# Opening of a hybrid encoder block: left halves of the first row tiles first, idle transposes between them, one operand split straight from PSUM, two differences on another engine

## The chip, the cores and the metric

The kernel runs on one core of one Trainium2 chip. The time is that of one execution on the device, in microseconds (us), and a kernel's time is the median of its runs. Five engines work beside each other: PE (TensorE, matrix products and transposes, with PEld for its weight loads), DVE (VectorE), ACT (ScalarE), POOL (GpSimd) and SP (SyncE, which here issues most of the transfers). Each carries out its own queue of instructions in order. PE writes to PSUM, which has eight banks of 128 x 512 float32 here; DVE and ACT read them, POOL does not.

## The reference

One encoder layer on 1024 tokens of width 1024. The change touches the input norm and the first columns of the combined projection.

```python
h = layer_norm(x, ln_in_g, ln_in_b)
for l in range(DEPTH):
    proj = h @ w_in[l]
    aq, ak, av, hq, hf_fwd, hf_bwd, hi, hg, ga, gh = jnp.split(proj, split_idx, axis=-1)
    att = dilated_attention(aq, ak, av, slopes)
    rec = hgrn2(hq, hf_fwd, hf_bwd, hi, hg, lower_bounds[:, l], hgrn_norm_g[l])
    merged = jax.nn.sigmoid(ga) * (att @ w_att_up[l]) + jax.nn.sigmoid(gh) * (rec @ w_hgrn_up[l])
    h = layer_norm(DEEPNORM_ALPHA * h + merged @ w_o[l], ln1_g[l], ln1_b[l])
    gate, up = jnp.split(h @ w_ffn_in[l], 2, axis=-1)
    h = layer_norm(DEEPNORM_ALPHA * h + (jax.nn.silu(gate) * up) @ w_ffn_out[l], ln2_g[l], ln2_b[l])
```

## The kernel before

**Products.** Every float32 operand of a product is split into a rounded high part and the rest, `hi` and `lo`, and a product is three matmuls: `w_hi` by `hi`, `w_hi` by `lo`, `w_lo` by `hi` (`mm3`, lines 270, 271 and 272 of the profile). A big product is done by Strassen's and Winograd's scheme with seven products of half size instead of eight. The projection's right operand is the normalised input, transposed, in four quarters: `b11` (features 0 to 511, tokens 0 to 511), `b21` (features 512 to 1023, same tokens), `b12` and `b22` (tokens 512 to 1023). Besides `b11`, `b21` and `b22` the scheme needs `t1` = b12 - b11, `t2` = b22 - t1, `t3` = b22 - b12 and `t4` = b21 - t2. Each is held as `xb11hi`, `xb11lo` and so on, in four slices of 128 features (k = 0 to 3). On the weights' side it needs the blocks a11 to a22 and their sums s1 to s4 (`sums`, lines 652 to 657: s1 = a21 + a22 and s2 = s1 - a11 on DVE, s3 = a22 - s2 on POOL, s4 = a12 - s2 on DVE).

**Order of the products.** `stream` makes the columns in groups of four tiles of 128, n = 0, 1, ...; a group has two halves g = 0, 1, and each of its seven products, numbered p = 1 (a11, b11), 2 (a12, b21), 6 (s2, t2), 5 (s1, t1), 7 (s3, t3), 3 (s4, b22) and 4 (a22, t4), takes 12 matmuls. The first two groups start together: p = 1 for n = 0 and 1, then p = 2 for both, and only then the rest of n = 0, then of n = 1. So p = 2 has four "b21 groups" of 12 matmuls: (n, g) = (0, 0), (0, 1), (1, 0), (1, 1). `prep` splits a product's weight, `w_hi` on ACT (line 212) and `w_lo` on POOL (line 222), three products ahead, into a ring of four; `leave` evacuates: `wkeep` copies on ACT (line 680), sums and `evh` on DVE and ACT (lines 542, 543, 556 to 558).

**The opening.** `phase0` makes the right operands while `stream`'s products run. Per row tile of 128 tokens (tt = 0 to 7, tile `xt`): `stats` on DVE (lines 348 to 350) and three small instructions on POOL (lines 351 to 353, tile `mv`), `norm` in place, half a row (q = 0 left, q = 1 right) per ACT instruction (line 331), `turn`, which transposes 128 x 128 pieces on PE (line 364) so that one PSUM bank (`sd`, four of them) gets one slice k of four row tiles. From these banks come: `w11`, the scaled b11 without its bias (`scaled`, line 376 on DVE, 331 on ACT), split to `b11`; `w21` (tile `v21`), split to `b21`; for the later four row tiles `t1` = bank - w11 (`less`, line 380, DVE), `z2` = bank - t1 and a scaled copy `w22` (ACT) from the right halves' banks; then the splits of t2 and t1, t3's difference (line 467, POOL, into w11's place), the splits of t3 and of b22 (both from SBUF), t4's difference (line 482, POOL) and its split. `hi` is an ACT instruction, `lo` a DVE instruction (lines 390, 391). `lent` names tiles that borrow the place of operands which are not made yet.

**What sets the order.** A scheduler orders each engine's queue by the place in the program and by priorities (evacuations ahead). Where `ordered` and `behind` are called, one instruction is held behind another in its queue without a wait: `xact` and `xdve` keep ACT's and DVE's instructions of the first half of the opening in the order written, and `gates` holds the first four weight casts behind given instructions. `run` lets `stream` go on by one product, so that its instructions stand there.

## Time and profile before

| | us |
|---|---|
| three runs | 2061.17, 2062.42, 2066.87 |
| median | 2062.42 |
| the profiled execution's own time | 2064.15 |
| its span | 2062.3 |
| first matmul of a product | 17.00 |
| first matmul of the second column group's p = 6 | 88.04 |

Rows of the timeline have the start in us, the time in us from the first one's start to the last one's end, engine, line, operation, what is written and read, shapes, the count of instructions merged, and in brackets how long the engine had been idle and what released it. An instruction's time holds the way through the engine too: matmuls of 0.39 us follow each other every 0.23 us. Rows of stages have the stretch, its length, the busy time (and count) of PE, PEld, DVE, ACT and POOL, the clock granted to PE as a share of the full one, the busy share of the DMA engines and GB/s.

### The profile page before, as it was taken

What the parts mean: (1) busy time and instruction counts of PE and PEld (TensorE: products, weight loads), DVE (VectorE), ACT (ScalarE), POOL (GpSimd) and SP (SyncE); (2) the same over time, 40 slices, a digit from 0 to 9 for tenths busy, and PEclk for the clock granted to TensorE, in tenths of its full rate; (3) what the DMA queues carried; (4) which work ended last, traced back from release to release, by engine and by line L of the source; (5) the groups of instructions that cost most, each with busy time, mean ns of one, the idle gap of its engine ahead of it and who ended that gap; (6) DMA issues with size and microseconds to landing.
All of it is one profiled execution on the core that took longest, in us unless ns stands there. A gap on an engine that the chain in (4) does not pass through costs nothing. (4 is left out here: it accounts for less than half of the span.)

```text
span 2062.3 us, 30940 instructions
## 1 busy us (share of the span) xinstructions
PE 2015.5 (98%) x10974; PEld 1670.5 (81%) x10974; DVE 1326.1 (64%) x2029; ACT 947.6 (46%) x1962; POOL 1063.9 (52%) x913
## 2 busy tenths in 40 slices
PE   7899999999999999999999999999999999999998
PEld 5688888788888888888888888787888888888886
DVE  6867645884377844677443225547777777767788
ACT  6554455553555536555365432244433333344541
POOL 5767644676446663666535652244656666630000
PEclk9999999999999999999999999999999999999999
DMA  5434533335334353344524376544544344358533
GB/s 158 133 115 142 171 119 105 128 129 177 116 127 132 114 177 98 121 131 145 165 95 150 123 247 204 183 133 125 171 131 141 127 149 137 108 170 298 160 96 128
DMA packets 274843, 297.94 MB, mean 144 GB/s; under 512 B 14017, under 2 KB 207362, under 8 KB 274690
## 3 DMA queue, kind: packets, MB, share of 16 engines
q1 hardware_dynamic: 268384, 274.78, 41.6%
q10 hardware_dynamic: 6306, 21.20, 2.7%
q8 instruction: 86, 1.41, 0.3%
q14 instruction: 67, 0.55, 0.1%
HBM read 201.29 MB, written 94.63 MB: 143 GB/s over the span
## 5 line engine op out<-in xcount | busy, mean ns | idle before, releaser
L222 POOL TENSOR_TENSOR w_lo<-wa,w_hi 128x512 fp32r<-128x512 f32 x272 | 362.6, 1341 | 274.7 <-ACT w_hi L212 259.7
L212 ACT CAST w_hi<-wa 128x512 fp32r<-128x512 f32 x272 | 168.4, 620 | 253.5 <-PE pj L271 146.8
L222 POOL TENSOR_TENSOR w_lo<-wsum,w_hi 128x512 fp32r<-128x512 f32 x88 | 128.0, 1464 | 111.7 <-PE sd L272 60.7
L222 POOL TENSOR_TENSOR w_lo<-f_raw,w_hi 128x512 fp32r<-128x512 f32 x66 | 102.5, 1561 | 53.2 <-ACT w_hi L212 51.8
L208 POOL TENSOR_TENSOR mv<-mv,mhalf 128x1 f32<-128x1 f32 x16 | 12.7, 797 | 218.9 <-DVE mv L207 218.1
L212 ACT CAST w_hi<-wsum 128x512 fp32r<-128x512 f32 x88 | 54.7, 621 | 122.2 <-PE sd L271 118.7
L542 DVE TENSOR_TENSOR evh<-wkeep,pj 128x512 f32<-128x512 f32 x45 | 30.9, 686 | 111.9 <-PE pj L272 63.2
L212 ACT CAST gwsum<-a_raw 128x512 fp32r<-128x512 f32 (+1 forms) x78 | 48.2, 618 | 112.6 <-PE pj L271 56.1
L270 PE MATMUL pj<-xt1hi,w_hi 128*128 128x512 f32 x252 | 99.6, 395 | 0.0
L270 PE MATMUL pj<-xb22hi,w_hi 128*128 128x512 f32 x252 | 99.1, 393 | 0.0
L272 PE MATMUL pj<-xb22hi,w_lo 128*128 128x512 f32 x252 | 98.2, 390 | 0.4 <-POOL w_lo L222 0.3
L271 PE MATMUL pj<-xb22lo,w_hi 128*128 128x512 f32 x252 | 98.6, 391 | 0.0
L272 PE MATMUL pj<-xt1hi,w_lo 128*128 128x512 f32 x252 | 98.5, 391 | 0.0
L271 PE MATMUL pj<-xt1lo,w_hi 128*128 128x512 f32 x252 | 98.4, 391 | 0.0
L654 POOL TENSOR_TENSOR wa<-wa,wa 128x512 f32<-128x512 f32 x46 | 67.1, 1467 | 40.4 <-DVE wa L653 35.5
L222 POOL TENSOR_TENSOR w_lo<-ws,w_hi 128x512 fp32r<-128x512 f32 x46 | 62.4, 1358 | 43.3 <-ACT w_hi L212 43.0
L680 ACT COPY wkeep<-pj 128x512 f32<-128x512 f32 x136 | 79.3, 583 | 7.8 <-PE pj L272 5.7
L531 DVE TENSOR_TENSOR evh<-wkeep,pj 128x512 f32<-128x512 f32 x66 | 57.8, 879 | 35.6 <-PE pj L272 25.1
L272 PE MATMUL pj<-xt2hi,w_lo 128*128 128x512 f32 x192 | 76.1, 396 | 4.1 <-POOL w_lo L222 4.1
L270 PE MATMUL pj<-xt2hi,w_hi 128*128 128x512 f32 x192 | 76.4, 401 | 1.1 <-ACT w_hi L212 1.1
L270 PE MATMUL pj<-xt4hi,w_hi 128*128 128x512 f32 x192 | 76.1, 396 | 0.8 <-ACT w_hi L212 0.8
L270 PE MATMUL pj<-xb11hi,w_hi 128*128 128x512 f32 x192 | 76.9, 402 | 0.0
(419 smaller groups left out, 6546.5 us busy)
## 6 DMA issues: line engine op xcount, KB each, us to landing
wa<-in_w_in_dram SPq DMA_DIRECT2D x184, 256.0 KB, 3.3
f_raw<-in_w_ffn_in_dram SPq DMA_DIRECT2D x44, 512.0 KB, 4.2
a_raw<-gd SPq DMA_DIRECT2D x30, 512.0 KB, 3.7
gd<-fc SPq DMA_DIRECT2D x44, 256.0 KB, 2.1
gd<-fs SPq DMA_DIRECT2D x33, 256.0 KB, 2.1
tg<-evh SPq DMA_DIRECT2D x32, 256.0 KB, 2.2
tg<-tg SPq DMA_DIRECT2D x16, 512.0 KB, 3.9
y<-ahs SPq DMA_DIRECT2D x16, 512.0 KB, 6.5
```

What stands on the lines that cost most here:

```text
L208: nc.gpsimd.tensor_tensor(mv[:, 2:3], mv[:, 2:3], self.mhalf[:, 0:1], OP.pow)
L212: ins = nc.scalar.copy(hi, src) if eng_hi == "act" else nc.vector.tensor_copy(hi, src)
L222: ins = e.tensor_sub(lo, src, hi.bitcast(F32))
L270: nc.tensor.matmul(ps, whi, xhi, start=first, stop=False, **kw)
L271: nc.tensor.matmul(ps, whi, xlo, start=False, stop=False, **kw)
L272: self.product = nc.tensor.matmul(ps, wlo, xhi, start=False, stop=last, **kw).ins.name
L531: self.left(nc.vector.tensor_tensor(o, self.order_src(add, g, kind), s, OP.add))
L542: self.left(nc.vector.tensor_add(t, add, ps))
L654: nc.gpsimd.tensor_sub(a["a21"], a["a22"], a["a11"])
L680: nc.scalar.copy(t, ps)
```

## The change

The opening alone is changed. In the loop over the first four row tiles only the first tile's right half is normalised on ACT; those of tiles 1 to 3 are written after the loop and go to DVE, as do the left halves of tiles 6 and 7 later. The first two weight casts are held behind the left-half norms of tiles 1 and 2. Between the left-half transposes stand 11, 7, 6 and 4 transposes of the identity into a place of a bank that is written later (`run_up`). The norms of tiles 4 to 7 are written left halves first. From each bank of tiles 4 to 7's left halves ACT now also copies the scaled b12 (`w12`); t3's difference is bank - w12 on DVE. b22 is split from PSUM: ACT writes its high part from the bank, then that part less the bias (`hb`, with `nbin`, the negated bias, made on POOL in the padding tile), and DVE writes the low part from bank and `hb`. t4's difference is on DVE. The sums s1 and s2 (and s3) of the first group's weights are put behind the first two slices of t1 (`later`).

```diff
@@ phase0
-        w11, t1, w22, z2 = (lent(z) for z in ("xb22hi", "xt3hi", "xt4hi", "xt4lo"))
+        w11, w12, t1, hb, z2 = (lent(z) for z in ("xb22hi", "xt4hi", "xt3hi", "xt3lo", "xt4lo"))
+        WARM = (11, 7, 6, 4)
+        nbin = self.spare[:, 0:4]
...
         def norm(tt, q):
             x, mv = xs[tt][:, HALF * q:HALF * (q + 1)], self.mv0[:, tt, :]
+            if tt > 5 and q == 0 or 0 < tt < 4 and q:
+                return dve(nc.vector.tensor_scalar(x, x, mv[:, 2:3], mv[:, 3:4], op0=OP.mult, op1=OP.add))
             return act(x, x, AF.Identity, bias=mv[:, 3:4], scale=mv[:, 2:3])
...
+        def run_up(n):
+
+            for i in range(n):
+                if 3 not in banks:
+                    banks[3] = self.ps_sd()
+                ins = nc.tensor.transpose(banks[3][:, 384:512], self.ident, self.ident)
+                if i == 0 and self.turned_last:
+                    self.behind(ins, self.turned_last)
+                self.turned_last = ins.ins.name
...
+        self.gates = [None] * 2
         for tt in range(4):
-            norm(tt, 0)
+            n = norm(tt, 0)
+            if 0 < tt < 3:
+                self.gates[tt - 1] = n.ins.name
+            run_up(WARM[tt])
             turn(tt, 0)
             if tt < 3:
                 stats(tt + 1)
+            if tt == 0:
                 norm(tt, 1)
+        for tt in range(1, 4):
+            norm(tt, 1)
         bias = [[column("bin", 4 * q + k) for k in range(4)] for q in range(2)]
+        nc.gpsimd.tensor_scalar(nbin, self.col["bin"][:, 4:8], -1.0, None, op0=OP.mult)
...
-        norm(3, 1)
         stats(4)
-        self.gates = [None] * 2 + [h.ins.name] * 2
+        self.gates += [h.ins.name] * 2
...
-        for tt in range(4, 8):
-            norm(tt, 0)
-            if tt < 7:
-                stats(tt + 1)
-            norm(tt, 1)
+        for tt in range(5, 8):
+            stats(tt)
+        for q in range(2):
+            for tt in range(4, 8):
+                norm(tt, q)
+        self.later = []
         run(3)
         for k in (0, 2):
             for tt in range(4, 8):
                 turn(tt, 0, (k, k + 1))
             for i in (k, k + 1):
-                less(t1, i, 0, w11)
+                scaled(w12, i, 0, True)
+                self.left(less(t1, i, 0, w11))
+            if k == 0:
+                for z in self.later:
+                    z()
+                self.later = None
             run()
+        self.forms("b22")
         for k in (0, 2):
...
             for i in (k, k + 1):
                 h = hi("t2", i, z2, bias[1][i]), lo("t2", i, z2, bias[1][i])
-                scaled(w22, i, 1, True)
+                parts.append(h)
+            for i in (k, k + 1):
+                ins = less(w12, i, 1, w12)
+                if i > k:
+                    self.behind(ins, parts[0][1].ins.name)
+                g, b, z = column("gin", 4 + i), bias[1][i], self.xb["b22"][0][:, i, :]
+                self.behind(act(z, banks[i], AF.Identity, bias=b, scale=g), h[0].ins.name)
+                act(hb[i], z.bitcast(F32), AF.Identity, bias=nbin[:, i:i + 1])
+                dve(nc.vector.scalar_tensor_tensor(self.xb["b22"][1][:, i, :], banks[i], g, hb[i], op0=OP.mult,
+                                                   op1=OP.subtract))
             run()
...
-        for k in range(4):
-            self.behind(nc.gpsimd.tensor_sub(w11[k], z2[k], w11[k]), last.ins.name)
...
-            hi("t3", k, w11, diff[:, k:k + 1])
-            last = lo("t3", k, w11, diff[:, k:k + 1])
-        run(2)
-        self.forms("b22")
+            hi("t3", k, w12, diff[:, k:k + 1])
+            last = lo("t3", k, w12, diff[:, k:k + 1])
+        run(3)
         for k in range(4):
-            hi("b22", k, w22, bias[1][k])
-            lo("b22", k, w22, bias[1][k])
-        run()
-        for k in range(4):
-            self.behind(nc.gpsimd.tensor_sub(w21[k], w21[k], z2[k]), last.ins.name)
+            self.behind(nc.vector.tensor_sub(w21[k], w21[k], z2[k]), last.ins.name)
@@ stream, sums
             n, g, p = seq[i]
             a = A[g]
+            if n == 0 and p == 6 and self.later is not None and not again:
+                self.later.append(lambda: sums(i, True))
+                return
```

How the queues stand where the prediction speaks of them. Line numbers of the changed kernel are its own (there line 372 is `turn`, 383 `run_up`).

PE's queue from the start of the program, before and with the change. `vrows` is the transpose of the norm's parameters, rows with `xt` are row tiles, rows without it the identity.

```order
L181 MATMUL sd<-tabs_sb,vrows_256 128x16
L364 MATMUL sd<-tabs_sb,xt 128x128 x22
L270 MATMUL pj<-xb11hi,w_hi 128x512 x2
L364 MATMUL sd<-tabs_sb,xt 128x128 x3
L271 MATMUL pj<-xb11lo,w_hi 128x512
```

```order
L183 MATMUL sd<-tabs_sb,vrows_257 128x16
L383 MATMUL sd<-tabs_sb 128x128 x11
L372 MATMUL sd<-tabs_sb,xt 128x128 x4
L383 MATMUL sd<-tabs_sb 128x128 x7
L372 MATMUL sd<-tabs_sb,xt 128x128 x4
L383 MATMUL sd<-tabs_sb 128x128 x6
L372 MATMUL sd<-tabs_sb,xt 128x128 x4
L383 MATMUL sd<-tabs_sb 128x128 x4
L372 MATMUL sd<-tabs_sb,xt 128x128 x12
L272 MATMUL pj<-xb11hi,w_hi 128x512 x2
L372 MATMUL sd<-tabs_sb,xt 128x128 x4
L273 MATMUL pj<-xb11lo,w_hi 128x512
```

28 transposes of the identity are added; of the right halves' transposes eight, not six, stand ahead of the first product.

POOL's queue from the last statistic of the third row tile to the first weight splits, before and with the change (`mv` is the statistic, three instructions a tile).

```order
L353 TENSOR_SCALAR mv_203<-mv_203 128x1
L351 TENSOR_SCALAR mv_203<-mv_203 128x1
L352 TENSOR_TENSOR mv_203<-mv_203,mhalf 128x1
L353 TENSOR_SCALAR mv_203<-mv_203 128x1
L222 TENSOR_TENSOR w_lo<-wa_259,w_hi 128x512
L222 TENSOR_TENSOR w_lo<-wa_261,w_hi 128x512
```

```order
L358 TENSOR_SCALAR mv_203<-mv_203 128x1
L356 TENSOR_SCALAR mv_203<-mv_203 128x1
L357 TENSOR_TENSOR mv_203<-mv_203,mhalf 128x1
L224 TENSOR_TENSOR w_lo<-wa_260,w_hi 128x512
L358 TENSOR_SCALAR mv_203<-mv_203 128x1
L224 TENSOR_TENSOR w_lo<-wa_262,w_hi 128x512
```

The first weight split now stands ahead of the last statistic of the fourth row tile.

DVE's queue from the evacuation of the second b21 group (`wkeep<-wkeep,sd`), before and with the change. `lent_xt4lo` is z2, `lent_xt3lo` hb, and `lent_xt4hi` holds w12 and then t3's difference.

```order
L556 TENSOR_TENSOR wkeep<-wkeep,sd 128x512
L380 SCALAR_TENSOR_TENSOR lent_xt4lo<-sd,vc,lent_xt3hi 128x512 x2
L558 SCALAR_TENSOR_TENSOR evh<-evh,wkeep 128x512
L391 SCALAR_TENSOR_TENSOR xt2lo<-lent_xt4lo,vc,xt2hi 128x512 x2
L556 TENSOR_TENSOR wkeep<-wkeep,sd 128x512
L380 SCALAR_TENSOR_TENSOR lent_xt4lo<-sd,vc,lent_xt3hi 128x512 x2
```

```order
L401 SCALAR_TENSOR_TENSOR lent_xt4lo<-sd,vc,lent_xt3hi 128x512
L596 SCALAR_TENSOR_TENSOR evh<-evh,wkeep 128x512
L594 TENSOR_TENSOR wkeep<-wkeep,sd 128x512
L412 SCALAR_TENSOR_TENSOR xt2lo<-lent_xt4lo,vc,xt2hi 128x512
L401 SCALAR_TENSOR_TENSOR lent_xt4hi<-sd,vc,lent_xt4hi 128x512
L401 SCALAR_TENSOR_TENSOR lent_xt4lo<-sd,vc,lent_xt3hi 128x512
L401 SCALAR_TENSOR_TENSOR lent_xt4hi<-sd,vc,lent_xt4hi 128x512
L412 SCALAR_TENSOR_TENSOR xt2lo<-lent_xt4lo,vc,xt2hi 128x512
L401 SCALAR_TENSOR_TENSOR lent_xt4lo<-sd,vc,lent_xt3hi 128x512
L596 SCALAR_TENSOR_TENSOR evh<-evh,wkeep 128x512
L504 SCALAR_TENSOR_TENSOR xb22lo<-sd,vc,lent_xt3lo 128x512
L412 SCALAR_TENSOR_TENSOR xt2lo<-lent_xt4lo,vc,xt2hi 128x512
```

The second piece begins behind three instructions that are not shown: the evacuation `wkeep`, a z2 and a t3 difference (in w12's place). With them the first `xb22lo` is the fourteenth instruction from that `wkeep` on, where before it was far outside this stretch; b22's bank is read until then.

More of the change, by code (lines that the diff above doesn't have):

```diff
@@ L125, in pad @@
         if n:
-            self.nc.gpsimd.memset(pool.tile([128, n // 4], F32, name=f"pad{n}"), 0.0)
+            t = pool.tile([128, n // 4], F32, name=f"pad{n}")
+            self.nc.gpsimd.memset(t, 0.0)
+            return t
     def ps_pj(self, i=None):
@@ L234, in ordered @@
         return ins
-    gone = gone2 = None
+    gone = gone2 = later = None
     def left(self, ins):
@@ L356, in norm @@
             x, mv = xs[tt][:, HALF * q:HALF * (q + 1)], self.mv0[:, tt, :]
+            if tt > 5 and q == 0 or 0 < tt < 4 and q:
+                return dve(nc.vector.tensor_scalar(x, x, mv[:, 2:3], mv[:, 3:4], op0=OP.mult, op1=OP.add))
             return act(x, x, AF.Identity, bias=mv[:, 3:4], scale=mv[:, 2:3])
         def turn(tt, q, ks=range(4)):
+            first = tt < 4 and q == 0
             for k in ks:
-                if tt % 4 == 0:
+                if tt % 4 == 0 and not (first and k in banks):
                     banks[k] = self.ps_sd()
-                nc.tensor.transpose(banks[k][:, 128 * (tt % 4):128 * (tt % 4) + 128],
-                                    xs[tt][:, 128 * (4 * q + k):128 * (4 * q + k) + 128], self.ident)
+                ins = nc.tensor.transpose(banks[k][:, 128 * (tt % 4):128 * (tt % 4) + 128],
+                                          xs[tt][:, 128 * (4 * q + k):128 * (4 * q + k) + 128], self.ident)
+                if first and k == 0:
+                    self.behind(ins, self.turned_last)
[6 more added lines that the diff above has]
+                if i == 0 and self.turned_last:
+                    self.behind(ins, self.turned_last)
+                self.turned_last = ins.ins.name
         def column(n, k):
@@ L378, in less @@
         def less(o, k, q, w):
-            dve(nc.vector.scalar_tensor_tensor(o[k], banks[k], column("gin", 4 * q + k), w[k], op0=OP.mult,
-                                               op1=OP.subtract))
+            return dve(nc.vector.scalar_tensor_tensor(o[k], banks[k], column("gin", 4 * q + k), w[k], op0=OP.mult,
+                                                      op1=OP.subtract))
         def hi(name, k, src, b=None):
@@ L642, in early, with sums @@
             return tc.high_priority(offset=self.evac_ahead if n > 1 else 0)
-        def sums(i):
+        def sums(i, again=False):
             if i >= len(seq):
```

5 lines of the change are left out of this document (4 added, 1 removed).

## The prediction

> **What bounds the kernel now.** I read the first part of the page, then the waits of TensorE (PE) by stage, then the opening instruction by instruction, because the diff touches nothing that runs after the first 100 us.
>
> ```profile
> span 2062.3 us, 30940 instructions
> PE 2015.5 (98%) x10974; PEld 1670.5 (81%) x10974; DVE 1326.1 (64%) x2029; ACT 947.6 (46%) x1962; POOL 1063.9 (52%) x913
> 0.00:200.00 200.00, 177.01 (x882) 142.89 (x883) 144.41 (x177) 109.71 (x203) 132.99 (x144) 0.97 0.44 138
> ...
> 1200.00:1400.00 200.00, 195.10 (x870) 160.29 (x869) 98.14 (x138) 64.98 (x101) 78.81 (x60) 0.99 0.57 184
> ```
>
> PE is busy for 98% of the span, so only its idle and slow stretches can be won. The stages (length, busy time of PE, PEld, DVE, ACT, POOL, granted clock, DMA share, GB/s) have 23 us without PE in the first 200 us; the worst later stretch of that length has 4.9. A product's matmul follows the one before after 0.23 us when nothing is late:
>
> ```profile
> 87.58 0.39 PE L271 MATMUL pj<-xt4lo,w_hi 128*128 128x512 f32 x1
> 87.81 0.39 PE L272 MATMUL pj<-xt4hi,w_lo 128*128 128x512 f32 x1
> 88.04 0.39 PE L270 MATMUL pj<-xt2hi,w_hi 128*128 128x512 f32 x1
> ```
>
> The matmul at 88.04 is the first of the second column group, and my finishing line: what the change gains before it is carried to the end, since PE hardly waits after 100 us. From the first product at 17.00 to that line PE loses time in five places:
>
> ```profile
> 17.00 1.20 PE L270 MATMUL pj<-xb11hi,w_hi 128*128 128x512 f32 x2
> 19.07 0.63 PE L272 MATMUL pj<-xb11hi,w_lo 128*128 128x512 f32 x1
> 19.50 0.63 PE L270 MATMUL pj<-xb11hi,w_hi 128*128 128x512 f32 x1
> 21.13 0.49 PE L364 MATMUL sd<-tabs_sb,xt 128*128 128x128 f32 x3
> 21.38 0.48 PE L271 MATMUL pj<-xb11lo,w_hi 128*128 128x512 f32 x1
> ...
> 34.24 0.39 PE L272 MATMUL sd<-xb21hi,w_lo 128*128 128x512 f32 x1
> 37.40 1.12 PE L364 MATMUL sd<-tabs_sb,xt 128*128 128x128 f32 x7 [2.03 <-DVE evh L542]
> 39.37 0.80 PE L270 MATMUL sd<-xb21hi,w_hi 128*128 128x512 f32 x1 [0.84 <-DVE lent_xt3hi L380]
> ...
> 58.66 0.39 PE L271 MATMUL sd<-xt1lo,w_hi 128*128 128x512 f32 x1
> 61.60 0.50 PE L271 MATMUL sd<-xt1lo,w_hi 128*128 128x512 f32 x1 [2.36 <-DVE xt1lo L390]
> 65.51 0.62 PE L270 MATMUL pj<-xt3hi,w_hi 128*128 128x512 f32 x2
> ...
> 73.24 0.39 PE L272 MATMUL pj<-xt3hi,w_lo 128*128 128x512 f32 x1
> 75.78 0.50 PE L271 MATMUL sd<-xb22lo,w_hi 128*128 128x512 f32 x1 [0.73 <-DVE xb22lo L391]
> 80.42 0.50 PE L270 MATMUL pj<-xt4hi,w_hi 128*128 128x512 f32 x1 [0.82 <-ACT w_hi L212]
> ```
>
> (1) 17.00 to 21.38: 8 matmuls and 6 transposes, 8 x 0.23 + 6 x 0.11 (three transposes took 0.49 at 21.13) = 2.5 us of work in 4.4: **1.9** lost, because a matmul follows after 0.43 us (19.07 to 19.50), at half speed. (2) 34.24 to 39.37: one matmul and ten transposes, 1.3 us of work: **3.8** lost, on the bank that the evacuation `evh` frees and on the difference `t1`. (3) The next 12 matmuls run slow again, 12 x 0.20 = **2.4**. (4) 58.66 to 65.51: nine matmuls and one transpose, 2.2 us: **4.6** lost, on `xt1lo` and on the slow clock after it. (5) 73.24 to 80.42: 15 matmuls, 3.4 us: **3.8** lost, on `xb22lo`. Together **16.5 us**.
>
> The clock, by stretches of 3.4 us:
>
> ```profile
> 14.20:17.62 3.42, 2.92 (x12) 2.43 (x13) 2.34 (x4) 2.82 (x5) 0.93 (x1) 1.00 1.16 311
> 34.69:38.10 3.41, 1.25 (x9) 1.01 (x10) 3.41 (x5) 3.41 (x7) 1.57 (x3) 1.00 0.02 5
> 38.10:41.52 3.42, 2.58 (x8) 1.83 (x7) 3.19 (x5) 0.83 (x2) 3.42 (x4) 0.50 0.21 77
> 62.00:65.41 3.41, 3.06 (x8) 1.95 (x7) 3.21 (x10) 1.48 (x3) 0.84 (x5) 0.50 0.91 261
> 75.65:79.06 3.41, 2.55 (x10) 1.76 (x11) 3.41 (x5) 0.89 (x2) 1.22 (x1) 1.00 0.00 0
> ```
>
> After a stretch with PE busy for 1.25 of 3.41 us the grant fell to 0.50; after 2.55 it stayed; 3.06 brought it back, 2.58 did not. At 14.20 the view still prints 1.00, but the 0.43 us pitch says half speed: before its first record the view cannot be trusted.
>
> **The change part by part.** *Left halves first.* Before, the left half of the fourth row tile waits behind right halves and two casts on ACT, until 13.69:
>
> ```profile
> 11.51 0.57 POOL L352 TENSOR_TENSOR mv<-mv,mhalf 128x1 f32<-128x1 f32 x1
> 12.18 0.26 POOL L353 TENSOR_SCALAR mv<-mv 128x1 f32<-128x1 f32 x1
> 12.40 1.28 POOL L222 TENSOR_TENSOR w_lo<-wa,w_hi 128x512 fp32r<-128x512 f32 x1
> 13.69 0.81 ACT L331 ACTIVATE xt<-xt,mv 128x512 f32<-128x512 f32 x1
> 14.56 2.79 PE L364 MATMUL sd<-tabs_sb,xt 128*128 128x128 f32 x10 [0.81 <-ACT xt L331]
> ```
>
> Its statistics were ready at 12.44. But the change's order on POOL has the split `w_lo` (1.28) ahead of the last statistic of that tile, and the new `nbin` (about 0.2, like the 0.26 row) ahead of all: 11.51 + 0.2 + 0.57 + 1.28 + 0.26 = 13.8. So ACT starts that tile at 13.8, not 13.7, and this part brings **nothing** to the first product (0.1 worse to 0.3 better by warm transposes; I take 0.2 better). What it does bring is later: the right halves of tiles 1 to 3 are off ACT, so the 16 right-half transposes end at about 19.5, not 25, and the `b21` splits no longer hold the later norms.
>
> *Idle transposes.* 28 more on PE, 0.21 us each when cold (the ten at 14.56 with their wait took 2.79), fitted between norms: 11 from 5.4 to 7.8, then 7, 6 and 4, the last ending by 14.0, before the norm at 14.6. They delay nothing. If they count as work, PE is busy 80% or more of 7.4 to 14.2 and the clock is up by 14.2; the next stretch (four transposes at 14.7, eight from 15.8, then products) has 2.3 of 3.4 us, near the 2.55 that kept it. Then loss (1), 1.9, goes. The nearest row cannot decide: 14.20 to 17.62 was 2.92 busy, nearly all transposes, and the clock stayed down, yet 2.92 lies between the 2.58 that failed and the 3.06 that served. I take 1.9; the bounds are 0 and 1.9.
>
> The Trainium skill, "TensorE: Matmul & The Clock Gate", Part 4 (PE-mode transpose), speaks against this part: transposes do not count as PE-busy the same way, and the full clock does not engage for them. By that rule loss (1) stays; no run here shows transposes alone for a whole stretch.
>
> *Second wait.* With products from 16.75 at full speed, 48 matmuls of `b11` and 16 transposes end at about 28.6 (now 31.0); the norms of tile 4 follow the `wkeep` copies on ACT and end at 29.1: 0.6 idle. The first `b21` group ends at 32.3 (now 34.5). POOL finishes tile 7's statistics behind two more `w_lo` at 33.15, DVE norms it by 33.6, PE turns it by 34.1; DVE makes `t1` in 0.7 and ACT, after the `evh` copy, the new `w12` by 35.2, both reading the bank that the second group needs. That group starts at 35.25, not 39.37: idle 0.2 + 1.15. Loss (2), 3.8, becomes 1.95. The weight sums (2.38 for two, next rows) stood ahead of the first `t1` on DVE and now stand behind it.
>
> ```profile
> 33.77 2.38 DVE L652 TENSOR_TENSOR ws<-wa,wa 128x512 f32<-128x512 f32 x2
> 38.57 2.71 DVE L380 SCALAR_TENSOR_TENSOR lent_xt3hi<-sd,vc,lent_xb22hi 128x512 f32<-128x512 f32 x4
> 50.60 6.42 POOL L467 TENSOR_TENSOR lent_xb22hi<-lent_xt4lo,lent_xb22hi 128x512 f32<-128x512 f32 x4
> 52.38 3.49 DVE L391 SCALAR_TENSOR_TENSOR xt2lo<-lent_xt4lo,vc,xt2hi 128x512 fp32r<-128x512 f32 x2
> 72.19 5.89 DVE L391 SCALAR_TENSOR_TENSOR xb22lo<-lent_xt4hi,vc,xb22hi 128x512 fp32r<-128x512 f32 x4
> ```
>
> PE is then never idle for 1.25 us in a row and stays above 50% busy in each stretch, so loss (3), 2.4, goes too.
>
> *DVE queue.* DVE instructions with both inputs in SBUF take 1.5 to 1.8 us beside POOL (52.38, 72.19), those that read PSUM 0.66 (38.57, POOL busy). `b22`'s low half now reads PSUM (4 x 0.8 saved), t3's difference is a DVE instruction on PSUM (4 x 0.66) instead of POOL's 6.42, t4's four cost DVE 2.7 instead of POOL's 5.5. But these all stand in one queue: from the end of the weight sums at 39.25, fourteen instructions to the first `xb22lo`, twelve of 0.67 and two beside POOL of 1.4, end at 39.25 + 8.0 + 2.8 = 50.0, less 0.3 overlap. Only that frees the bank of the last `b21` group. PE waits on the way, by the same count: 1.3 for the bank of the last right-half transposes, 0.85 and 1.35 for `xt2lo`, 0.6 for `xb22lo`: **4.1 new**. In return `xt1lo` is there by 55.2 when PE wants it from 55.1 on, and the last `xb22lo` by 60.0 when PE wants it from 66 on: losses (4) and (5), 4.6 + 3.8, go. `nbin`, `hb` and the two more bank reads by ACT lie beside this DVE queue; were DVE free, ACT's 4 x 0.7 + 4 x 0.6 would be next.
>
> **Sum**: 16.5 - 0.6 - 1.35 - 4.1 + 0.2 = 10.7 us, less about 1.0 for 15 hand-overs of 0.06 (13.69 + 0.81 = 14.50, PE at 14.56) that the count above leaves out: **9.7**. Beyond the line stand four waits, 1.1 + 1.3 + 0.4 + 1.2 between starts:
>
> ```profile
> 89.63 0.50 PE L272 MATMUL pj<-xt2hi,w_lo 128*128 128x512 f32 x1 [0.97 <-POOL w_lo L222]
> 93.30 0.50 PE L270 MATMUL pj<-xt2hi,w_hi 128*128 128x512 f32 x1 [1.11 <-ACT w_hi L212]
> 97.09 0.50 PE L272 MATMUL pj<-xt2hi,w_lo 128*128 128x512 f32 x1 [1.02 <-POOL w_lo L222]
> ```
>
> They hang on loads that casts of the first group release, and so move along with PE: taken as unchanged, bounds 4 us won (all gone) and 4 us lost (doubled). The profiled execution took 2064.15 us, 1.7 above the median of the three runs (2062.42) and inside their spread; the gain is taken from the median: 2062.4 - 9.7 = **2052.7**.
>
> **Rivals.** *The transposes do not lift the clock*: loss (1) stays, 2054.6. For it: the stretch at 14.20. Against: that stretch was not full. By the skill's rule named above, this is what happens. *The second group still starts cold*: PE is 45 to 55% busy around 35, between the 1.25 that dropped the clock and the 2.55 that kept it, above all if the first rival holds too: 2.4 more, 2055.1 to 2057.0. *The loads bind*: PE is 10 us earlier at a line where weights already come 1 us late; if the four waits double and one of 2 to 5 us joins them, 2058 to 2062, and much of the change buys nothing. Against it: DMA is idle (0.00 to 0.02 busy) in two of the stretches above. *Slower, the DVE queue*: if each of the fourteen instructions took the 1.75 of the row at 52.38, the last `b21` group would start at 39.25 + 24.5 = 63.8 instead of 49.7; 14.1 lost against 9.7, 2066.8. It decides from a mean of 0.77 + 9.7/14 = 1.46 us. Against: nine of the fourteen read PSUM, and POOL has eight subtractions fewer. *The order does not do what it says* (left halves early) holds for the first product, and is in the sum.
>
> **How the numbers follow.** Forecast 0.42; clock not lifted 0.25; second group cold 0.13; loads 0.12; DVE queue 0.08. A measurement here tells 0.3% (6.2 us) from no change: faster means below 2056.2. Forecast and first rival lie below (0.63 of their 0.67), half of the third (0.06): 0.69. The loads, the rest of these three and half of the DVE case lie within: 0.25. Slower takes the other half of the DVE case and what I have not thought of: 0.06. The forecast's own range is 2049 to 2056; 8 in 10 reaches up through the loads to 2061, and down by the 4 us of the later waits and some of the hand-overs to 2047.5.
>
> **What would show it.** In the changed profile: the fourth left half on ACT still at 13.7 to 13.9; the pitch of the first product's matmuls, 0.23 (clock lifted) or 0.43; the second `b21` group at about 35, its matmuls 0.39 long, not 0.63; waits of 0.5 to 1.5 us for `xt2lo` and `xb22lo` between 42 and 50; no wait for `xt1lo` near 60 nor `xb22lo` near 75; the second column group's first matmul near 78. I am wrong if that line comes after 84, if a wait of over 3 us stands ahead of the last `b21` group, or if PE loses more than 6 us between this line and 100.

## The result, and the profile after

The changed kernel takes 2056.49 us (median of 20 runs, 2051.56 to 2062.08), the kernel before 2062.11 us (20 runs, 2058.50 to 2066.87): a ratio of 0.9973, with a 95% interval of 0.9965 to 0.9981. The gain is 5.6 us; forecast were 9.7.

The head of the changed kernel's page, then PE's timeline (columns as before; `turn` is line 372 and `mm3` lines 272 to 274 here):

```profile
span 2049.8 us, 31004 instructions
PE 2011.1 (98%) x11002; PEld 1668.8 (81%) x11002; DVE 1321.7 (64%) x2042; ACT 947.6 (46%) x1961; POOL 1058.8 (52%) x906
```

```profile
16.77 0.71 PE L272 MATMUL pj<-xb11hi,w_hi 128*128 128x512 f32 x2
...
18.68 0.39 PE L274 MATMUL pj<-xb11hi,w_lo 128*128 128x512 f32 x1
18.90 0.39 PE L272 MATMUL pj<-xb11hi,w_hi 128*128 128x512 f32 x1
...
28.46 0.39 PE L274 MATMUL pj<-xb11hi,w_lo 128*128 128x512 f32 x1
30.40 0.44 PE L372 MATMUL sd<-tabs_sb,xt 128*128 128x128 f32 x2 [1.55 <-ACT xt L336]
...
35.55 0.66 PE L372 MATMUL sd<-tabs_sb,xt 128*128 128x128 f32 x4 [0.49 <-DVE xt L363]
37.70 0.79 PE L272 MATMUL sd<-xb21hi,w_hi 128*128 128x512 f32 x1 [1.49 <-DVE lent_xt3hi L401]
38.29 0.63 PE L273 MATMUL sd<-xb21lo,w_hi 128*128 128x512 f32 x1
...
52.63 0.47 PE L272 MATMUL sd<-xb21hi,w_hi 128*128 128x512 f32 x1 [0.35 <-DVE xb22lo L504]
...
80.56 0.39 PE L272 MATMUL pj<-xt2hi,w_hi 128*128 128x512 f32 x1
```

The first product runs at 0.23 us a matmul at once. The waits for `xt1lo` and the late `xb22lo` are gone. The wait ahead of the second b21 group is not (37.70), and its first matmuls follow each other after 0.43 us (38.29, next at 38.71), at half speed. The line, the first matmul of the second column group, comes at 80.56 instead of 88.04, 7.5 us earlier. All of that is won behind the last b21 group: it starts at 52.63, 1.5 us later than before (51.16), but from there to the line are 27.9 us instead of 36.9. Little of it is lost behind the line: counted by what they read, the same matmuls start 7.1 us earlier at 134 us (127.10 instead of 134.20) and still at 300 us.

The profiled executions differ by 12.3 us (2064.15 against 2051.88), much more than the medians. The windows show why, before first (columns as in the prediction):

```profile
1330.00:1350.00 20.00, 17.10 (x68) 13.40 (x68) 7.40 (x13) 6.09 (x11) 6.59 (x10) 0.91 0.37 108
1435.00:1460.00 25.00, 22.86 (x90) 17.66 (x89) 19.54 (x22) 13.65 (x21) 12.59 (x9) 0.93 0.66 201
```

```profile
1320.00:1340.00 20.00, 17.71 (x81) 14.09 (x80) 7.59 (x15) 7.26 (x12) 6.87 (x10) 1.00 0.45 136
1425.00:1450.00 25.00, 22.44 (x94) 17.35 (x95) 22.16 (x22) 13.67 (x20) 14.61 (x10) 1.00 0.67 205
```

In code that the change does not touch, the execution before lost the full clock twice and the one after did not: the distance grows from 8.3 us at 1287 to 12.3 at 1464. One execution against another compares such luck as well; the line and the medians compare the change.

### The profile page after: what moved, and what is told of

Read it like the earlier page. It is cut to its first block, busy times and chain, and to the rows that moved or that the text cites. A ratio compares the mean times of both kernels' runs of the same rounds, so it can differ in the third digit from the quotient of the medians.

```text
span 2049.8 us, 31004 instructions
## 1 busy us (share of the span) xinstructions
PE 2011.1 (98%) x11002; PEld 1668.8 (81%) x11002; DVE 1321.7 (64%) x2042; ACT 947.6 (46%) x1961; POOL 1058.8 (52%) x906
## 5 line engine op out<-in xcount | busy, mean ns | idle before, releaser
L274 PE MATMUL pj<-xt3hi,w_lo 128*128 128x512 f32 x192 | 75.5, 393 | 1.9 <-POOL w_lo L224 1.8
L273 PE MATMUL pj<-xt2lo,w_hi 128*128 128x512 f32 x192 | 75.9, 395 | 1.4 <-DVE xt2lo L412 1.4
L224 DVE TENSOR_TENSOR gwkeep<-a_raw,gwsum 128x512 fp32r<-128x512 f32 (+1 forms) x78 | 53.2, 682 | 36.7 <-ACT gwsum L214 33.9
```

Source lines behind the costliest of these rows:

```text
L224: ins = e.tensor_sub(lo, src, hi.bitcast(F32))
L273: nc.tensor.matmul(ps, whi, xlo, start=False, stop=False, **kw)
L274: self.product = nc.tensor.matmul(ps, wlo, xhi, start=False, stop=last, **kw).ins.name
```

## The experiments

Line numbers of kernels with added lines are a few higher. In the table: start of the first product, of the second, third and last b21 group and the line, in the profiled execution; then the median with its count of runs, and the ratio to the kernel before. The kernels stand in the order in which they ran: each four from after_again on shared a chip and the runs of the kernel before.

| kernel | first product | 2nd b21 | 3rd b21 | last b21 | line | median (runs) | ratio, 95% |
|---|---|---|---|---|---|---|---|
| before | 17.00 | 39.37 | 45.59 | 51.16 | 88.04 | 2062.11 (20) | |
| changed | 16.77 | 37.70 | 42.84 | 52.63 | 80.56 | 2056.49 (20) | 0.9973 [0.9965, 0.9981] |
| after_again | 18.45 | 39.35 | 44.47 | 54.28 | 82.16 | 2055.28 (8) | 0.9966 [0.9955, 0.9978] |
| no_idle | 17.74 | 36.61 | 40.39 | 52.25 | 81.77 | 2057.30 (11) | 0.9979 [0.9968, 0.9989] |
| stat_first | 15.55 | 36.92 | 42.16 | 51.85 | 79.76 | 2054.68 (6) | 0.9952 [0.9937, 0.9967] |
| stat_late | 17.53 | 36.85 | 40.52 | 51.77 | 79.69 | 2052.78 (6) | 0.9953 [0.9938, 0.9967] |
| stat_both | 15.71 | 34.34 | 39.58 | 49.27 | 77.18 | 2052.15 (6) | 0.9948 [0.9935, 0.9962] |
| diffs_pool | 17.20 | 37.93 | 41.56 | 51.14 | 86.40 | 2060.05 (12) | 0.9989 [0.9978, 0.9999] |
| b22_sbuf | 17.09 | 38.01 | 43.25 | 47.99 | 82.72 | 2056.38 (8) | 0.9973 [0.9960, 0.9985] |
| idle_4 | 17.71 | 39.47 | 43.12 | 54.38 | 82.25 | 2057.80 (12) | 0.9973 [0.9963, 0.9984] |
| sums_early | 17.73 | 42.15 | 47.70 | 55.76 | 85.30 | 2058.53 (10) | 0.9979 [0.9970, 0.9989] |
| halves_back | 16.31 | 36.73 | 40.51 | 52.55 | 81.93 | 2058.37 (11) | 0.9979 [0.9970, 0.9988] |
| both_swap | 15.69 | 33.51 | 37.15 | 47.11 | 76.67 | 2051.14 (5) | 0.9939 [0.9926, 0.9953] |
| both_swap_n7 | 15.63 | 35.07 | 40.31 | 49.46 | 79.01 | 2054.75 (5) | 0.9960 [0.9948, 0.9973] |

**after_again**: the changed kernel, nothing edited.

> The changed kernel once more, as the mark for the runs beside it. Its twenty times lay between 2051.6 and 2062.1 us, wider than those of the kernel before (most within 2060.7 to 2062.9), and its profiled execution was one of the fastest (2051.88). If the spread comes from where the 3.4 us grid of the clock falls on the half-idle stretch around 34 to 38 us, another profile has the same waits to within 0.3 us but another count of slow matmuls, there or in a later half-idle stretch. If it comes from the loads, the waits for weights behind 80 us differ by microseconds. Median 2055 to 2058 by both.

Neither. The waits are the same to 0.2 us; the whole opening is later, because the load of the second row tile landed later. DVE's first statistics of that tile, in the first profile and in this one:

```profile
6.54 1.29 DVE L353 BATCH_NORM_STATS2 bn<-xt 128x6 f32<-128x512 f32 x2 [0.63 <-DMA xt<-in_x_dram]
```

```profile
8.20 1.29 DVE L353 BATCH_NORM_STATS2 bn<-xt 128x6 f32<-128x512 f32 x2 [2.47 <-DMA xt<-in_x_dram]
```

From 6.54 to 8.20 are 1.66 us; first product, second b21 group and line are 1.68, 1.65 and 1.60 later. In every other profiled execution of the table this row starts between 6.49 and 6.83, so the other rows can be compared with the changed kernel's as they stand. One source of the spread is shown, then: the first loads. Whether the kernel before spreads less for that reason stays open.

**POOL's queue.** The statistics of a row tile end with three small instructions on POOL. What the changed kernel's queue did with them:

```profile
12.28 1.26 POOL L224 TENSOR_TENSOR w_lo<-wa,w_hi 128x512 fp32r<-128x512 f32 x1
13.64 0.27 POOL L358 TENSOR_SCALAR mv<-mv 128x1 f32<-128x1 f32 x1
...
23.98 1.30 POOL L224 TENSOR_TENSOR w_lo<-wa,w_hi 128x512 fp32r<-128x512 f32 x1 [1.54 <-PE pj L274]
...
25.87 1.30 POOL L224 TENSOR_TENSOR w_lo<-wa,w_hi 128x512 fp32r<-128x512 f32 x1
...
29.23 0.27 POOL L358 TENSOR_SCALAR mv<-mv 128x1 f32<-128x1 f32 x1
...
32.57 1.46 POOL L224 TENSOR_TENSOR w_lo<-wfirst,w_hi 128x512 fp32r<-128x512 f32 x1
...
34.65 0.27 POOL L358 TENSOR_SCALAR mv<-mv 128x1 f32<-128x1 f32 x1
```

The fifth tile's statistic is there at 29.50, behind two splits, and the eighth's at 34.92, behind four. Three kernels hold the splits back by order alone (`HOLD` names the row tile for each split by its number: 0 and 1 behind tile 3, or 4 behind tile 4 and 5 to 7 behind tile 7, or all):

```diff
-            nc.gpsimd.tensor_scalar(mv[:, 3:4], mv[:, 0:1], mv[:, 2:3], -1.0, op0=OP.mult, op1=OP.mult)
+            ins = nc.gpsimd.tensor_scalar(mv[:, 3:4], mv[:, 0:1], mv[:, 2:3], -1.0, op0=OP.mult, op1=OP.mult)
+            self.done[tt] = ins.ins.name
...
         ins = e.tensor_sub(lo, src, hi.bitcast(F32))
+        if self.HOLD.get(self.splits) in self.done:
+            self.behind(ins, self.done[self.HOLD[self.splits]])
+        self.splits += 1
```

> The changed kernel with POOL's first two weight splits held behind the last statistic of the fourth row tile (a hold of order, without a wait). In the profile of the changed kernel that statistic stood behind the split from 12.28 to 13.54, and the norm of the fourth left half began at 13.94. POOL theory: the norm begins at about 12.7, the first product at 15.6 to 15.8 instead of 16.77, and since the split then ends at 14.1 nothing waits for it; of the 1.0 to 1.2 us a part reaches the end, because the wait for the fifth tile's statistic (30.40) keeps its place: median 2055.5 to 2056.5. Rival: the first product waits for something else (its weights or the right halves on DVE), and it moves by less than 0.4 us.

The first product starts at 15.55, as the POOL theory said, and the line is 0.8 us earlier. The medians alone (2054.7 and 2055.3, six and eight runs spread over 7 to 9 us) would not show it.

> The changed kernel with POOL's fifth weight split held behind the statistics of the fifth row tile and the sixth to eighth splits behind those of the eighth. In the profile of the changed kernel that last statistic came at 34.92 with three splits ahead of it. POOL theory: it comes at about 30 us, the wait of 1.55 ahead of the first b21 group falls to under 0.5, the second b21 group starts at 34 to 34.5 instead of 37.70 and at full speed, the last b21 group 2 to 3.5 us earlier than 52.63, and the median falls by 2 to 4.5 us to 2052 to 2054.5. Rival, the DVE queue binds: the second b21 group starts earlier, but the last one still waits for xb22lo within 1 us of 52.6, and the median stays within 1 us of 2056.5. Second rival: the splits that come later keep the b21 groups waiting for w_lo, and nothing is won.

The wait ahead of the first b21 group is gone and the statistic is there at 31.0, but the second b21 group starts at 36.85, not at 34: it now waits 1.96 us for t1, which waits for the copy `w12` on ACT, and all that stands ahead of it is late. In this execution the clock fell just before the first product. The changed kernel's stretch there held 1.76 us of PE's work; the stretch of this kernel, at other boundaries, held 1.50, and in the next one the grant is 0.50:

```profile
13.61:17.02 3.41, 1.76 (x13) 1.52 (x14) 3.08 (x4) 2.63 (x4) 1.49 (x2) 1.00 1.22 309
```

```profile
12.30:15.71 3.41, 1.50 (x12) 1.02 (x10) 1.77 (x2) 1.56 (x3) 2.73 (x3) 1.00 1.11 324
15.71:19.12 3.41, 3.21 (x13) 2.91 (x14) 2.88 (x5) 3.34 (x7) 0.00 (x0) 0.50 1.13 334
```

The last matmul of `b11` starts at 29.96 instead of 28.46, 1.5 us later. The line is 0.9 us earlier in spite of that, so the line alone undersells this hold.

> Both holds on POOL together: first splits behind the fourth tile's statistic, later splits behind the eighth's. Alone, the first brought the first product to about 1.2 us earlier, and the second took away the wait ahead of the first b21 group, but the second b21 group then waited for ACT (evh copy, then the copy w12, then t1 on DVE). If POOL is what the prediction had wrong: the line (first matmul of the second column group) 1.5 to 2.5 us earlier than the changed kernel's in a run with the same first loads (80.56), median 2052.5 to 2054. If ACT and DVE behind it bind anyway, the line gains no more than the 1.2 us of the first hold, median 2054 to 2055.5.

Both together: line 77.18, 3.4 us earlier than the changed kernel's (1.5 to 2.5 were expected), and 2052.15 us. POOL theory holds, and the distance from the start of the last `b11` matmul to the second b21 group shows it apart from the clock's luck ahead of it: 9.24 us in the changed kernel (8.86 to 9.67 in after_again, stat_first, b22_sbuf and idle_4, which leave these splits where they are), 6.89 in stat_late, 6.93 here. The late hold is worth about 2.3 us, and the first brings the last `b11` matmul forward by 1.05 (28.46 to 27.41). PE and POOL of this kernel:

```profile
34.34 0.76 PE L277 MATMUL sd<-xb21hi,w_hi 128*128 128x512 f32 x1 [1.98 <-DVE lent_xt3hi L407]
```

```profile
29.23 0.28 POOL L363 TENSOR_SCALAR mv<-mv 128x1 f32<-128x1 f32 x1
29.47 1.29 POOL L224 TENSOR_TENSOR w_lo<-wa,w_hi 128x512 fp32r<-128x512 f32 x1
```

The eighth tile's statistic is there at 29.5, 5.4 us earlier, and nothing waited for the splits; yet 1.98 us of the old wait stand. What holds it, in the changed kernel's ACT and DVE:

```profile
35.67 0.61 ACT L581 ACTIVATE evh<-evh 128x512 f32<-128x512 f32 x1
36.19 2.40 ACT L336 ACTIVATE lent_xt4hi<-sd,vc 128x512 f32<-128x512 f32 x4
```

```profile
36.89 1.41 DVE L401 SCALAR_TENSOR_TENSOR lent_xt3hi<-sd,vc,lent_xb22hi 128x512 f32<-128x512 f32 x2 [1.39 <-ACT lent_xt4hi L336]
```

t1 does not read `w12`, only the same bank, and it starts when the first `w12` ends (36.19 + 0.7). **both_swap** writes t1 ahead of `w12`, and **both_swap_n7** also gives the eighth tile's right half to DVE:

```diff
-                scaled(w12, i, 0, True)
                 self.left(less(t1, i, 0, w11))
+                scaled(w12, i, 0, True)
```

```diff
-            if tt > 5 and q == 0 or 0 < tt < 4 and q:
+            if tt > 5 and q == 0 or 0 < tt < 4 and q or tt == 7:
```

> Both holds on POOL, and in each slice t1 (DVE) written ahead of the copy w12 (ACT), so that t1 no longer waits for ACT's queue and w12 follows t1 in the same bank. With both holds alone the second b21 group waited 1.98 us (to 34.34) behind the transposes, for t1 behind w12 behind evh's copy on ACT, and that idle stretch dropped the clock. If that chain is what is left: the second b21 group 0.5 to 1 us earlier, at full speed when PE is busy for over 1.75 us of its 3.4 us stretch, line 75.5 to 76.8 instead of 77.18, median 2050 to 2052. Rival: ACT's queue (right-half norms) ends last in either order, nothing moves, median 2052 to 2053.

DVE in stat_both and in both_swap, then both_swap's waits on PE:

```profile
33.53 1.41 DVE L407 SCALAR_TENSOR_TENSOR lent_xt3hi<-sd,vc,lent_xb22hi 128x512 f32<-128x512 f32 x2 [1.88 <-ACT lent_xt4hi L341]
```

```profile
31.67 1.40 DVE L407 SCALAR_TENSOR_TENSOR lent_xt3hi<-sd,vc,lent_xb22hi 128x512 f32<-128x512 f32 x2
```

```profile
33.51 0.50 PE L277 MATMUL sd<-xb21hi,w_hi 128*128 128x512 f32 x1 [1.05 <-ACT lent_xt4hi L341]
43.11 0.50 PE L278 MATMUL pj<-xt2lo,w_hi 128*128 128x512 f32 x1 [2.04 <-DVE xt2lo L418]
...
56.26 0.50 PE L279 MATMUL sd<-xt1hi,w_lo 128*128 128x512 f32 x1 [1.86 <-POOL w_lo L224]
```

t1 starts 1.9 us earlier, and with it DVE's whole queue: the last b21 group is 2.2 us earlier in spite of a new wait for `xt2lo`. A new wait for a weight split (56.26) then takes most of it back: line 76.67. This is the fastest kernel of the study, 2051.14 us, 4 to 5 us below the changed kernel; from stat_both it cannot be told by its time.

> As both_swap, with the right half of the eighth row tile normalised on DVE, which sits idle there, instead of ACT. If ACT's right-half norm ahead of evh's copy and w12 holds the chain (0.72 us of ACT's time): the second b21 group another 0.5 to 0.8 us earlier than in both_swap, median 2049.5 to 2051.5. Rival: DVE, now late with evh or t1 itself, gives it back: no difference from both_swap within 0.5 us at the line.

A miss: DVE comes to `evh` only behind the added norm, PE's last transposes wait 1.46 us for it, and the line falls back to 79.01.

**The idle transposes.** `no_idle` has the first of the two new lines, `idle_4` the second:

```diff
-        WARM = (11, 7, 6, 4)
+        WARM = (0, 0, 0, 0)
+        WARM = (0, 0, 0, 4)
```

> The changed kernel without the 28 transposes of the identity. If they lift the clock: the granted clock's first record comes after 17 us instead of at 10.2 us, the first product's matmuls follow each other after 0.43 us up to about 20 us, and everything behind is 1.5 to 2 us later, median about 2058.3. The rival, the rule that transposes do not lift the clock: they do nothing, the clock came up through the products themselves, and the same kernel without them starts its second product at the same time within 0.3 us, median unchanged (2056.5).

> The changed kernel with only the last four of its 28 transposes of the identity; here the queues of ACT, DVE and POOL are the changed kernel's, which they were not without all 28. If transposes count for the clock: its first record at full clock comes at 17 to 21 us instead of about 10, part of the first product runs at 0.43 us a matmul, and the line is 0.5 to 1.9 us later, median 2056 to 2057.5. If they do not, the clock comes up as before and nothing moves.

PE and a window of the changed kernel, then windows of after_again, then PE and windows of idle_4:

```profile
5.23 2.61 PE L383 MATMUL sd<-tabs_sb 128*128 128x128 f32 x11
...
11.13 0.82 PE L383 MATMUL sd<-tabs_sb 128*128 128x128 f32 x6
```

```profile
6.78:10.19 3.41, 3.07 (x15) 2.67 (x15) 3.35 (x9) 1.95 (x3) 2.14 (x9) 1.00 1.13 361
```

```profile
8.40:11.81 3.41, 1.41 (x11) 0.97 (x9) 3.38 (x9) 0.62 (x2) 1.73 (x7) 1.00 0.97 267
11.81:15.23 3.42, 2.94 (x14) 2.94 (x15) 1.63 (x4) 2.26 (x4) 3.15 (x5) 0.50 0.81 272
```

```profile
20.36 0.39 PE L272 MATMUL pj<-xb11hi,w_hi 128*128 128x512 f32 x1
20.59 0.39 PE L273 MATMUL pj<-xb11lo,w_hi 128*128 128x512 f32 x1
```

```profile
13.46:16.88 3.42, 2.64 (x12) 1.84 (x11) 2.79 (x3) 2.31 (x4) 1.60 (x3) 1.00 1.22 301
```

Transposes alone lifted the clock: eleven took 2.61 us at 5.23, six 0.82 at 11.13, and no product had run. In idle_4 the stretch up to 16.88 held 2.64 us of work, and only at 20.36 is the pitch 0.23; the first product is 0.9 us later, the line 1.7. `no_idle`, 1.2 us later at the line, also moved other queues (the second b21 group is earlier, and a wait of 3.12 us for `xt2lo` is new at 47.51), so only idle_4 measures the part: 1.7 us in one execution. The medians do not show it apart from the spread.

**The other parts undone, one at a time.** `diffs_pool`:

```diff
-        w11, w12, t1, hb, z2 = (lent(z) for z in ("xb22hi", "xt4hi", "xt3hi", "xt3lo", "xt4lo"))
+        w11, t1, hb, z2 = (lent(z) for z in ("xt4hi", "xt3hi", "xt3lo", "xt4lo"))
...
-                scaled(w12, i, 0, True)
...
-                ins = less(w12, i, 1, w12)
...
+            self.behind(nc.gpsimd.tensor_sub(w11[k], z2[k], w11[k]), last.ins.name)
...
-            self.behind(nc.vector.tensor_sub(w21[k], w21[k], z2[k]), last.ins.name)
+            self.behind(nc.gpsimd.tensor_sub(w21[k], w21[k], z2[k]), last.ins.name)
```

> The changed kernel with t3's and t4's differences back on POOL, made from SBUF, and without the copies w12 on ACT. w12 theory: in the changed kernel t1 of each slice waits for the copy w12 of the same bank, so w12 stands in the chain to the second b21 group, and 4 + 4 instructions of 0.66 us stand in DVE's queue up to the end of the splits: without them the second b21 group starts 0.7 to 1.3 us earlier than 37.70 (seen from the end of the transposes: 1.2 us behind instead of 2.0), the last b21 group at 49.5 to 51 instead of 52.63; what comes back is POOL's 4 x 1.6 us for t3 behind the last split of t1, so that w_hi by xt3 starts late or a weight split of POOL is late around 62 to 72: 1 to 3 us lost there. Median 2054 to 2057. Rival, the differences on DVE were the gain: the last b21 group no earlier, and a wait of over 2 us for xt3lo, median 2058 or more.

Both theories had a part. Without `w12` PE waits 0.52 us for t1 instead of 1.49, and the last b21 group is 1.5 us earlier. But POOL's four subtractions take 6.83 us, DVE's splits beside them 1.7 us each, and PE waits for `xt1lo`; the clock then stays down for 10 us (last fence). DVE, POOL, PE and the windows:

```profile
53.65 3.48 DVE L411 TENSOR_TENSOR xt1lo<-lent_xt3hi,xt1hi 128x512 fp32r<-128x512 f32 x2
```

```profile
49.74 6.83 POOL L508 TENSOR_TENSOR lent_xt4hi<-lent_xt4lo,lent_xt4hi 128x512 f32<-128x512 f32 x4
```

```profile
61.16 0.80 PE L273 MATMUL sd<-xt1lo,w_hi 128*128 128x512 f32 x1 [2.56 <-DVE xt1lo L411]
```

```profile
57.22:60.63 3.41, 1.39 (x6) 0.78 (x5) 3.41 (x4) 2.63 (x5) 2.71 (x3) 1.00 0.13 37
60.63:70.87 10.24, 9.37 (x20) 6.04 (x21) 9.94 (x14) 3.79 (x7) 7.17 (x9) 0.50 0.47 143
```

The differences on DVE carry most of the gain: 5.8 us at the line (86.40 against 80.56), some 4 in the median. Here too the clock fell ahead of the first product and the last matmul of `b11` came 1.6 us late; how much of that is in the 5.8 is not shown. What follows the last b21 group is not touched by it: 35.3 us to the line instead of 27.9.

`b22_sbuf`:

```diff
-                self.behind(act(z, banks[i], AF.Identity, bias=b, scale=g), h[0].ins.name)
-                act(hb[i], z.bitcast(F32), AF.Identity, bias=nbin[:, i:i + 1])
-                dve(nc.vector.scalar_tensor_tensor(self.xb["b22"][1][:, i, :], banks[i], g, hb[i], op0=OP.mult,
-                                                   op1=OP.subtract))
+                self.behind(act(hb[i], banks[i], AF.Copy, scale=g), h[0].ins.name)
+                hi("b22", i, hb, b)
+                lo("b22", i, hb, b)
```

> The changed kernel with b22 split from a scaled copy in SBUF again (one ACT copy from the bank, then hi on ACT and lo on DVE from SBUF), everything else as changed. In the changed kernel the bank of the last b21 group is held until the first xb22lo at 51.75. If reading from PSUM is a gain by itself: lo takes 0.75 to 1.7 us each beside POOL instead of 0.66, and the last xb22lo comes later than the p = 3 products want it; median 2057.5 or more. If it only moved the hold: the bank comes free with ACT's copy, the last b21 group starts 0.5 to 2 us earlier, xb22lo is still there long before 70, and the median falls by 0 to 1.5 us to 2054 to 2056.

The bank comes free as the second theory said, and by more (last b21 group at 47.99, 4.6 us earlier), and it buys nothing (line 2.2 us later, the same median): the first `xb22lo` from SBUF takes 1.78 us instead of 0.74, stands ahead of `xt2lo`, and PE waits there.

```profile
58.33 0.50 PE L273 MATMUL pj<-xt2lo,w_hi 128*128 128x512 f32 x1 [1.92 <-DVE xt2lo L412]
```

`sums_early`:

```diff
-        self.later = []
         run(3)
...
-            if k == 0:
-                for z in self.later:
-                    z()
-                self.later = None
```

> The changed kernel without the deferral: the sums s1 and s2 of the first group's weights stand again where they were written, one pair ahead of t1 on DVE and one between the slices of t1. In the changed kernel DVE waits from 35.5 to 36.9 with nothing to do, for ACT's copy w12, so the sums ahead of t1 would fall into waits. By the prediction's own reasoning (the sums ahead of the first t1 cost the second b21 group 2.4 us): the second b21 group 1 to 2.4 us later, median 2057 to 2058.5. Rival: they fall into DVE's idle time, the second b21 group stays within 0.5 us, and what they no longer take behind t1 brings the last b21 group 0.5 to 1.3 us earlier; median 2054.5 to 2056.

The second b21 group is 4.5 us later, more than either theory said. Of these, 1.7 us are there at the first b21 group (32.31 against 30.60): the clock fell ahead of the first product as in stat_late, after a stretch with 1.47 us of PE's work. The rest is not for DVE's sums: POOL makes s3 and its split, 2.5 us, as soon as s2 is there, ahead of the eighth tile's statistic.

```profile
36.09 1.27 POOL L690 TENSOR_TENSOR wa<-wa,wa 128x512 f32<-128x512 f32 x1
...
37.84 1.26 POOL L224 TENSOR_TENSOR w_lo<-wa,w_hi 128x512 fp32r<-128x512 f32 x1
39.20 0.27 POOL L358 TENSOR_SCALAR mv<-mv 128x1 f32<-128x1 f32 x1
```

`halves_back`:

```diff
-            if tt > 5 and q == 0 or 0 < tt < 4 and q:
+            if tt > 5 and q == 0:
...
-            if tt == 0:
                 norm(tt, 1)
...
         lo("b11", 3, w11, bias[0][3])
+        norm(3, 1)
```

> The changed kernel with the right halves of the first four row tiles normalised on ACT, in the loop and behind the b11 splits, as before. By the prediction: the first product starts at the same time to within 0.7 us (that part brings nothing to it), and the right halves' transposes end later (21 to 25 us instead of 19.7), which delays the b21 splits but not PE, which has b11 to multiply until 28.7; the line within 1 us of the changed kernel's, median 2055.5 to 2057.5. Rival: the moved halves are worth more, because ACT is late with b21's splits and so with the norms of the fifth row tile: the wait ahead of the first b21 group grows by 1 to 2 us, median 2057.5 to 2058.5.

The first product is 0.5 us earlier, as expected to within the bound. The line is 1.4 us later and the median lies in the rival's range, but not by the rival's way: the wait ahead of the first b21 group shrank (0.79), and PE waits 3.13 us for `xt2lo` at 47.64, because DVE's queue came out in another order. What the halves are worth by themselves stays open.

## Why the prediction was right, and where it was wrong

**Bounds and line.** The time is 3.8 us above the forecast, 0.5 above the forecast's own range (2049 to 2056) and inside the wider one (2047.5 to 2061). The five losses were the right ones: (1), (4) and (5) went. Of 9.7 us at the line (88.04 to 78.3) 7.5 came. Of these, 7.1 stand from 134 to 300 us, and the medians show 5.6; what the difference is in stays open, since the line is read from one execution of each kernel.

**First product.** Right: norm of the fourth left half at 13.94, first product at 16.77 (forecast 16.75), end of `b11` at 28.7 (28.6). That POOL's split stood ahead of the statistic was seen, and stat_first shows that it cost 1.2 us.

**Clock, loss (1).** Right: 1.9 taken, 1.7 measured with idle_4. But it was closer than the forecast knew, and in the profile luck had a part. The stretch that runs into the first product was forecast at 2.3 us of work and held 1.76; 1.50 in stat_late let the clock fall. Eleven of the profiled executions had all 28 transposes, and three of them (stat_late, diffs_pool, sums_early) lost the clock there and came to the end of `b11` 1.5 to 1.6 us late. The rival that the transposes do not lift the clock, and the rule behind it in the Trainium skill ("TensorE: Matmul & The Clock Gate", Part 4: PE-mode transpose), do not hold for the float32 transposes here: six took 0.82 us after a stretch of nothing but transposes.

**Second wait, loss (2): the step that failed.** "The norms of tile 4 follow the wkeep copies on ACT and end at 29.1" and "POOL finishes tile 7's statistics behind two more w_lo at 33.15": POOL's queue was counted for the last tile alone. The fifth tile's statistic came at 29.50, because a split that waited 1.54 us for its place stood ahead of it: PE lost 1.7 us between two starts instead of 0.6. The eighth tile's came at 34.92. The second b21 group started 2.45 us later than forecast. stat_both puts POOL right, and its second group starts 6.93 us behind the start of the last `b11` matmul; the forecast's distance is 6.9 (35.25 less 28.4). So POOL's queue accounts for this miss. stat_both reaches a line of 77.18 and 2052.15 us, near the forecast's 78 and 2052.7, but 1.05 us of it by an earlier first product, which the forecast did not have.

That t1 stands behind `w12` is then no part of the miss, but a further gain: with t1 ahead, in both_swap, the same distance is 6.15. That two engines' readings of one bank are put one behind the other could have been read: the Trainium skill says that the compiler's scheduler adds a dependency between any two instructions on different engines that touch the same bank and quadrant, reads too ("PSUM — Partial Sum Buffer", section "PSUM bank collisions raise a hardware error"), and the trace agrees (t1 at 36.89, when the first `w12` ends).

**Cold second group, loss (3).** The stretch from 34.09 held 1.50 us of PE's work, 44% where the forecast had PE busy for more than half of each stretch; the clock fell, and seven matmuls ran slow; the rival with a chance of 0.13 came true. Its price did not: it was set at 2.4, and was nothing. The table shows it: from the second b21 group to the third are 5.1 to 5.2 us where it ran cold (changed, after_again, stat_first, stat_both) and 3.7 where it did not (stat_late, idle_4), but from the second to the last are 14.9 us in all six. What sets the last group is DVE, busy for 15.38 of the 15.60 us from the first t1:

```profile
34.09:37.50 3.41, 1.50 (x10) 0.79 (x8) 1.52 (x3) 2.79 (x6) 0.73 (x2) 1.00 0.10 39
36.89:52.49 15.60, 13.06 (x54) 9.63 (x54) 15.38 (x23) 10.47 (x17) 7.58 (x5) 0.89 0.09 35
```

**DVE queue.** Right in mechanism and size: the forecast had 14.45 us from the second b21 group to the last (35.25 to 49.7), and 14.93 came. From there to the line it had 28.6 (to 78.3) and 27.9 came. So the missing 2.2 us at the line are 2.45 + 0.5 - 0.7: the second wait is the whole of it, and the two other differences nearly cancel. As DVE's queue starts with t1, what delays t1 delays the line; this is why the holds on POOL are worth so much.

**Beyond the line.** Taken as unchanged, and nearly so: from the line to the same matmul near 130 us it takes 46.5 us (80.56 to 127.10) instead of 46.2 (88.04 to 134.20), 0.4 lost. The loads rival did not come true.

**What the prediction undersaid.** The differences on DVE were charged for their 2.7 us and credited only through losses (4) and (5); diffs_pool shows them as the part that carries the gain (from the last b21 group to the line 35.3 us again, against 27.9). `b22` from PSUM is worth 2.2 us at the line of one execution and nothing that the medians show.

## What to carry to other kernels

Where a tiny instruction gates a long chain, look at what stands ahead of it in its engine's queue, and at what that in turn waits for: here a hold of order without any wait was worth 3.4 us at the line, where the whole change had won 7.5. A part that is undone alone can move the order of four queues; compare the queues before believing its time. Compare milestones in the stage that was changed beside the medians, since one execution's total holds the luck of first loads and of the clock; a milestone holds it too, so take the distance between two of them.

## What the runs showed of the hardware

In these traces the clock changes at boundaries 3.41 us apart and goes with how long PE was busy in the stretch before, and transposes count. At half speed a stretch of 2.64 us of work (idle_4) or 2.92 (before, from 14.20) did not lift it; 2.94 (after_again, from 11.81) and 3.07 did, but 3.12 (diffs_pool, from 64.04) did not. At full speed 1.39, 1.41 and 1.50 dropped it and 1.76 kept it; 1.64 dropped it in b22_sbuf (from 35.58) and kept it in sums_early (from 29.21). So near these borders the profile's busy time does not settle it. The boundaries fall elsewhere in every run: in idle_4 the same wait ahead of the second b21 group (1.49 us, as in the changed kernel) was split between two stretches, and the clock stayed:

```profile
33.94:37.35 3.41, 2.80 (x18) 1.98 (x16) 1.79 (x3) 2.80 (x4) 2.56 (x5) 1.00 0.01 2
37.35:40.77 3.42, 1.93 (x10) 1.47 (x11) 2.11 (x4) 3.01 (x6) 0.00 (x0) 1.00 0.23 81
```
